# Other start addresses for the tiles that TensorE's split products read

## The chip, the core and the metric

The kernel runs as one program on one core of a Trainium2 chip. The metric is the device time of one execution in microseconds, the median of several executions. The core's engines are TensorE (PE, matrix products; its weight loads are listed apart, as PEld), VectorE (DVE), ScalarE (ACT), GpSimd (POOL) and SyncE (SP, which issues the large DMAs). SBUF is the on-chip memory that the engines read; in each of its 128 partitions a tile begins at a byte address, which the program's allocator sets when the program is built.

## What is computed

Three transformer-like blocks, one after the other, on 256 tokens of width 1024 in float32. Cut to the products that matter here:

```python
# block 1, twice: feed-forward, mixer (chunked_sgu or pool_mixer), feed-forward
x = x + 0.5 * (silu(rmsnorm(x) @ w_gate) * (rmsnorm(x) @ w_up)) @ w_out     # 1024 -> 2816 -> 1024
x = x + (u * gate(v)) @ w_out            # chunked_sgu: u, v = split(gelu(rmsnorm(x) @ w_in))
x = x + (grouped(pooled(p)) * scale) @ w_out      # pool_mixer: p = rmsnorm(x) @ w_in
# block 2: attention (two kinds), then a mixture of experts, 32 experts, 4 for each token
x = x + gt1 * rms_norm(concat(y_mla, y_dsa) @ w_o)
x = x + gt2 * rms_norm(moe_ffn(h2, w_router, w_mlp1, w_mlp2))
# block 3: stick-breaking attention and state-space branch, cross attention, convolution feed-forward
x = x + rms_norm(merged @ w_out)
x = x + rms_norm(memory_cross_attention(h, mem_n) )
x = x + rms_norm((gelu(gate) * val) @ w_down)     # gate, val = split(conv(h @ w_up)), 1024 -> 2816 -> 1024
```

## The kernel before

**Split products.** Outside the experts, a float32 product is made of three TensorE products of type float32r. Each operand is split into a high part (rounded, by ScalarE, line 163 or 192) and a low part (what is left, by VectorE, line 164 or 193). `mm3` (line 178) multiplies high by high, high by low, and low by high, into one PSUM bank:

```python
mm(out, whi, xhi, start=start, stop=False, skip_group_check=True)     # line 180
mm(out, whi, xlo, start=False, stop=False, skip_group_check=True)     # line 181
mm(out, wlo, xhi, start=False, stop=stop, skip_group_check=True)      # line 182
```

The first operand is loaded into the array as weights (128 x 128), the second moves past it (128 x 256, one column for each token). Every product has a weight load of its own. There are 3,862 calls of `mm3`, so 11,586 products; all but 246 of them have 256 columns.

**Where the operands lie.** `xhi` and `xlo` (the normalised input of a stage, 8 pieces of 256 columns each) are in the pool `const` from line 43 on, and stay at one place for the whole program. A stage's weights come by DMA into `rawp` (10 slots of 8 KB a partition) and are split into a tile `hi` of 8 KB from the ring `splitp` (`parts`, line 309): high part in the first half, low part in the second. Some stages add ring slots on the right-hand end of SBUF, in the pool `splitr` (`rings`, line 68). What the first layer of a feed-forward stage leaves is split into small tiles `ahi` and `alo` (128 x 256) from a pool that the stage opens itself, so their address depends on what was allocated before it: `ffna` in `ffn`, `sgu3` in `sgu`, `pm3` in `pool_mixer`, `mx1` in `mix3`, `xa2` in `cross`, `cv` in `conv_ffn`. A tile of weights and a piece of `xhi` are multiples of 512 bytes long, so within a stage a product's two addresses, taken modulo 512, are the same for every piece.

**Order.** A feed-forward stage takes one column tile of 128 of the hidden layer after the other: 48 products with `xhi`, `xlo` as the moving operand (8 pieces, gate and up, three each), then 24 with `ahi`, `alo` of an earlier tile (8 column tiles of the output, three each). The weights of the tiles to come are split meanwhile. The order on TensorE is that of the program; it does not depend on addresses. Every 36 to 70 us in block 1's feed-forward stages a side job (line 692, part of block 2's conditioning) puts other products between two tiles.

Of the kernel before, what the change touches and what calls it, by code (L numbers as in the profile page):

```python
# [12 lines left out]
F32 = mybir.dt.float32  # L13
F32R = mybir.dt.float32r
# [5 lines left out]
P = 128  # L20
T = 256
D = 1024
KT = D // P
# [18 lines left out]
class Net:  # L42
    def __init__(self, ctx, tc, I):
        self.ctx, self.tc, self.nc, self.I = ctx, tc, tc.nc, I
        self.uid = 0
        pool = lambda name, bufs, **kw: ctx.enter_context(tc.tile_pool(name=name, bufs=bufs, **kw))
        self.const = pool("const", 1)
        self.psum = pool("psum", 8, space=PSUM)
        self.small = pool("small", 2)
        self.rawp = pool("rawp", 10, reuse_waits="tile")  # L50
        self.ring_size, self.ring_scope, self.right_scope, self.latest = None, None, None, ()
        self.rings(8)
        nc = self.nc
        self.ident = self.const.tile([P, P], F32, name="ident")
        make_identity(nc, self.ident)
        self.ones = self.const.tile([P, 1], F32, name="ones")
        nc.vector.memset(self.ones, 1.0)
        self.mhalf = self.const.tile([P, 4], F32, name="mhalf")
        nc.vector.memset(self.mhalf, -0.5)
        self.xT = self.const.tile([P, KT, T], F32, name="xT")  # L60
        self.xhi = self.const.tile([P, KT, T], F32R, name="xhi")
        self.xlo = self.const.tile([P, KT, T], F32R, name="xlo")
# [5 lines left out]
    def rings(self, split, right=0, left=0):  # L68

        if self.right_scope is not None:  # L70
            self.right_scope.close()
        self.right_scope = ExitStack()
        if self.ring_size != split:
            if self.ring_scope is not None:
                self.ring_scope.close()
            self.ring_size = split
            self.ring_scope = ExitStack()
            if split:
                self.splitp = self.ring_scope.enter_context(self.tc.tile_pool(name=self.nm("splitp"), bufs=split, reuse_waits="tile"))
        self.turn_of = [self.splitp] * split  # L80
        for n, side in ((right, "right"), (left, "left")):
            if n:
                more = self.right_scope.enter_context(self.tc.tile_pool(name=self.nm("splitr"), bufs=n, reuse_waits="tile", side=side))
                self.turn_of += [more] * n

    def nm(self, s):
        self.uid += 1
        return f"{s}_{self.uid}"
# [220 lines left out]
    def parts(self, a, b, slot=False):  # L309
        if slot:  # L310
            t = self.slot(F32R).rearrange("p (z n) -> p z n", z=2)
        else:
            self.turn_of.append(self.turn_of.pop(0))
            t = self.turn_of[-1].tile([P, 2, 1024], F32R, tag="hi", name=self.nm("hi"))
        return tuple(t[:, z, :a * b].rearrange("p (a b) -> p a b", a=a) for z in range(2))

    def ahead(self, makers, n):
# [79 lines left out]
    def ffn(self, w_in, w_out, nxt, side, pieces=False, ready=(), fill=()):  # L397
        nc = self.nc
        F = D_FF // P
        wave = 2  # L400
        with self.tc.tile_pool(name=self.nm("ffna"), bufs=3) as ap_:
            raw, W, WO = {}, {}, {}

            def fetch(c):
# [97 lines left out]
    def sgu(self, w_in, w_s, b_s, w_out, vg, nxt):  # L502
        nc = self.nc
        A2 = 2048
        with self.tc.tile_pool(name=self.nm("sgu1"), bufs=1) as p1, \
                self.tc.tile_pool(name=self.nm("sgu3"), bufs=3) as p3:
            v = [self.slot() for _ in range(2)]
            bs = p1.tile([P, 8, P], F32, name=self.nm("bs"))
            nc.gpsimd.dma_start(bs, b_s.partition_broadcast(P))
# [20 lines left out]
            for c in range(4):  # L530
                pv = [self.bank(), self.bank()]
                for u in range(4):
                    hi, lo = get()
# [58 lines left out]
    def pool_mixer(self, w_in, w_grp, scale, w_out, nxt):  # L592
        nc = self.nc
        Z = 16
        with self.tc.tile_pool(name=self.nm("pm1"), bufs=1) as p1, \
                self.tc.tile_pool(name=self.nm("pm3"), bufs=3) as p3:
            inv = p1.tile([P, 4, Z], F32, name=self.nm("inv"))
            for g in range(4):
                w = 2 << g
# [77 lines left out]

    def ada_jobs(self, scratch, c, w, b, mod):
        nc = self.nc
        sc = self.const.tile([P, KT], F32, name=self.nm("sc"))  # L680

        parts = scratch.tile([4, 48, P], F32, name=self.nm("parts"))

        def job(i):
            if i == 0:
                nc.scalar.activation(sc, c(), AF.Silu)
            ps = self.bank()
            for q in range(2):
                raw = self.raw(w[512 * q:512 * (q + 1), 512 * i:512 * (i + 1)], 4, 512)
                for z in range(4):  # L690
                    k = 4 * q + z
                    nc.tensor.matmul(ps[32 * z:32 * z + 32, :], sc[:, k:k + 1].to_broadcast([P, 32]), raw[:, z, :],
                                     start=q == 0, stop=q == 1, tile_position=(0, 32 * z), skip_group_check=True)
            row = self.small.tile([P, 512], F32, tag="adarow", name=self.nm("adarow"), bufs=1)
            nc.scalar.copy(row, ps)
            for z in range(4):
                nc.gpsimd.dma_start(parts[z:z + 1, 4 * i:4 * i + 4, :].rearrange("z r m -> z (r m)"), row[32 * z:32 * z + 1, :])

        got = []

        def load():
            rows = self.small.tile([48, 4, P], F32, tag="adarow", name=self.nm("adarows"), bufs=1)
            got.append(rows)
            nc.gpsimd.dma_start(rows, parts.rearrange("z r m -> r z m"))

        def end():

            pt, rows = self.bank(), got[0]
            for z in range(4):
                nc.tensor.matmul(pt[:, 0:48], rows[:, z, :], self.ident[0:48, 0:48], start=z == 0, stop=z == 3, skip_group_check=True)  # L710
            nc.vector.tensor_tensor(mod, pt[:, 0:48], b(), op=ALU.add)

        return [lambda i=i: job(i) for i in range(12)] + [load, end]
# [1329 lines left out]
    def mix3(self, V, w_in, w_glu, w_a, w_s, w_out, nxt, units, ahead):  # L2043
# [3 lines left out]
        xhi, xlo = lambda k: self.xhi[:, k, :], lambda k: self.xlo[:, k, :]  # L2047
        with self.tc.tile_pool(name=self.nm("mx1"), bufs=1, reuse_waits="tile") as p1, \
                self.tc.tile_pool(name=self.nm("mx4"), bufs=2, reuse_waits="tile") as pg:
            so = p1.tile([P, 2, 4, T], F32R, name=self.nm("so"))  # L2050
            ao = p1.tile([P, 2, 4, T], F32R, name=self.nm("ao"))
            rb, r2 = None, None
            wg, gt = {}, {}
            with self.tc.tile_pool(name=self.nm("mx2"), bufs=1, reuse_waits="tile") as q1, \
# [182 lines left out]
                for i0 in (0, 2):  # L2237
                    hi, lo = self.unit(raws["glu"][:, :, i0 * P:(i0 + 2) * P])
# [65 lines left out]
    def cross(self, V, wq, wo, nxt, units, ahead):  # L2304
        nc = self.nc
        mm = nc.tensor.matmul
        with self.tc.tile_pool(name=self.nm("xa1"), bufs=1, side="right", reuse_waits="tile") as p1, \
                self.tc.tile_pool(name=self.nm("xa2"), bufs=2) as p2:
            self.rings(4, 1)
            mk = p1.tile([P, KT, T], F32, name=self.nm("mk"))  # L2310
            nc.sync.dma_start(mk, self.mk)
# [62 lines left out]
    def conv_ffn(self, V, w_up, w_down, nxt, units):  # L2374
# [3 lines left out]
        wave = 2  # L2378
        cw, cb = V["conv_w"], V["conv_b"]
        with self.tc.tile_pool(name=self.nm("cv"), bufs=3) as ap_:  # L2380
            raw, W, WO, gu, A = {}, {}, {}, {}, {}

            for i, unit in enumerate(units):
# [468 lines left out]
```

## Time and profile before

| | |
|---|---|
| median of 3 executions | 2688.53 us (2688.33 to 2691.99) |
| the profiled execution, its own time | 2696.91 us |
| its span, first to last instruction | 2695.2 us |
| mean granted TensorE clock | 0.948 of full speed |
| TensorE busy | 2443.8 us, 91% of the span |
| weight loads busy | 1863.6 us |
| VectorE, ScalarE, GpSimd busy | 1343.3, 918.1, 254.0 us |
| DMA | 716.20 MB, mean 266 GB/s |

How it is read: the span falls into stages. From 0 to 985 us are block 1's feed-forward stages and mixers, to 1210 us block 2's attention, to 2180 us the experts, to 2440 us the first part of block 3, to 2500 us its cross attention, and then the convolution stage. A TensorE row's busy time overlaps the next one's, because products are pipelined; what a product takes from the stage is the step from its start to the next one's start, which is read from the rows in order of time.

### The profile page before, as it was taken

Reading aid. Unit: us, or ns where it says so; the run is one execution under the profiler, and the core shown is the slowest. Engines: PE = TensorE matmul, PEld = TensorE weight load, DVE = VectorE, ACT = ScalarE, POOL = GpSimd, SP = SyncE. Lnnn points to the kernel's source line nnn. Section 1 sums busy time; section 2 is a strip of 40 time slices with the busy share of each in tenths; the row PEclk is TensorE's granted clock in tenths of the full one; section 3 lists DMA queues with packets and bytes.
Section 4 is the critical chain, followed back from the end, with each engine's and each line's share of the span. In section 5 each row is a group of like instructions: output and inputs, shape, how many; then the busy total and the mean of one; then the engine's idle time right before and its main releaser. Section 6 shows DMA issues by size and latency. Waiting matters only on the chain. (4 is left out here: it accounts for less than half of the span.)

```text
span 2695.2 us, 42836 instructions
## 1 busy us (share of the span) xinstructions
PE 2443.8 (91%) x17207; PEld 1863.6 (69%) x17207; DVE 1343.3 (50%) x2786; ACT 918.1 (34%) x1531; POOL 254.0 (9%) x444
## 2 busy tenths in 40 slices
PE   7999999999999999999889888789777787999998
PEld 7998999999999998784333333223222156998997
DVE  5556677577777775942111111111111059766875
ACT  4445454454445444531100100001010042555653
POOL 0011000110021102220000000000000027111000
PEclk8999999999999999999989989899999798999999
DMA  7956455676737652449999999999999973444640
GB/s 240 325 181 201 158 195 196 211 254 219 235 126 266 207 178 97 142 183 367 419 413 420 416 415 418 420 420 419 420 419 419 419 268 110 157 162 136 218 142 17
DMA packets 274116, 716.20 MB, mean 266 GB/s; under 512 B 15023, under 2 KB 179354, under 8 KB 223610
## 3 DMA queue, kind: packets, MB, share of 16 engines
q1 hardware_dynamic: 269370, 703.63, 69.8%
q0 software_dynamic: 4544, 9.80, 1.1%
q8 instruction: 136, 2.23, 0.3%
q14 instruction: 66, 0.54, 0.1%
HBM read 703.84 MB, written 9.54 MB: 265 GB/s over the span
## 5 line engine op out<-in xcount | busy, mean ns | idle before, releaser
L182 PE MATMUL b<-xhi,hi 128*128 128x256 f32 x2392 | 681.5, 285 | 15.7 <-DVE hi L164 15.6
L180 PE MATMUL b<-xhi,hi 128*128 128x256 f32 x2392 | 685.9, 287 | 6.0 <-ACT xhi L192 4.9
L181 PE MATMUL b<-xlo,hi 128*128 128x256 f32 x2392 | 680.8, 285 | 4.6 <-DVE xlo L193 2.4
L164 DVE TENSOR_TENSOR hi<-raw,hi 128x1024 fp32r<-128x1024 f32 (+3 forms) x517 | 605.9, 1184 | 157.5 <-ACT hi L163 152.7
L163 ACT CAST hi<-raw 128x1024 fp32r<-128x1024 f32 (+3 forms) x517 | 509.7, 1003 | 510.4 <-PE b L182 458.4
L180 PEld LDWEIGHTS b<-xhi,hi 128*128 128x128 f32 x2392 | 460.3, 192 | 19.5 <-ACT hi L163 7.8
L182 PEld LDWEIGHTS b<-xhi,hi 128*128 128x128 f32 x2392 | 460.1, 192 | 18.2 <-DVE hi L164 18.0
L181 PEld LDWEIGHTS b<-xlo,hi 128*128 128x128 f32 x2392 | 460.3, 192 | 6.5 <-DVE xlo L193 4.5
L1477 DVE TENSOR_SCALAR g<-b 128x256 f32<-128x256 f32 x48 | 20.3, 422 | 596.1 <-PE b L1496 331.8
L180 PE MATMUL b<-ahi,hi 128*128 128x256 f32 x1072 | 303.4, 284 | 1.8 <-ACT ahi L163 1.7
L181 PE MATMUL b<-alo,hi 128*128 128x256 f32 x1072 | 302.3, 282 | 2.2 <-DVE alo L164 1.3
L182 PE MATMUL b<-ahi,hi 128*128 128x256 f32 x1072 | 301.7, 282 | 0.0
L181 PEld LDWEIGHTS b<-alo,hi 128*128 128x128 f32 x1072 | 203.4, 190 | 3.2 <-DVE alo L164 2.2
L180 PEld LDWEIGHTS b<-ahi,hi 128*128 128x128 f32 x1072 | 203.1, 190 | 3.0 <-ACT ahi L163 2.9
L182 PEld LDWEIGHTS b<-ahi,hi 128*128 128x128 f32 x1072 | 203.5, 190 | 0.0
L1480 ACT ACTIVATE sg<-g 128x256 f32<-128x256 f32 x48 | 20.0, 416 | 525.5 <-DVE g L1477 525.5
L1528 PE MATMUL b<-raw,xe 128*64 128x512 f32 x648 | 153.1, 609 | 16.6 <-DMA raw<-in_w_mlp_dram 16.6
L1496 PE MATMUL b<-raw,xe 128*32 128x512 f32 x928 | 124.9, 650 | 35.3 <-DMA raw<-in_w_mlp_dram 35.0
L1577 ACT COPY y<-b 64x512 f32<-64x512 f32 x68 | 39.4, 579 | 249.4 <-PE b L1570 241.6
L1528 PEld LDWEIGHTS b<-raw,xe 128*64 128x64 f32 x648 | 42.6, 138 | 118.1 <-issue 74.4
L452 DVE TENSOR_TENSOR t<-b,rb 128x256 f32<-128x256 f32 x88 | 37.1, 422 | 167.2 <-PE b L182 167.1
L1496 PEld LDWEIGHTS b<-raw,xe 128*32 128x32 f32 x928 | 24.1, 112 | 118.6 <-DMA raw<-in_w_mlp_dram 75.7
(662 smaller groups left out, 3278.7 us busy)
## 6 DMA issues: line engine op xcount, KB each, us to landing
raw<-in_w_mlp_dram SPq DMA_DIRECT2D x275, 1024.0 KB
wb<-in_w_mlp_dram SPq DMA_DIRECT2D x108, 1024.0 KB
raw<-in_ffn_w_in_dram SPq DMA_DIRECT2D x84, 1024.0 KB
raw<-in_ffn_w_out_dram SPq DMA_DIRECT2D x44, 1024.0 KB
raw<-in_w_ada_dram SPq DMA_DIRECT2D x24, 1024.0 KB
raw<-in_ffn_w_up_dram SPq DMA_DIRECT2D x22, 1024.0 KB
raw<-in_w_in_dram SPq DMA_DIRECT2D x21, 1024.0 KB
raw<-in_a_w_in_dram SPq DMA_DIRECT2D x16, 1024.0 KB
```

What stands on the lines that cost most here:

```text
L163: a = self.nc.scalar.copy(hi, src)
L164: return a.ins, self.nc.vector.tensor_tensor(lo, src, hi.bitcast(F32), op=ALU.subtract).ins
L180: mm(out, whi, xhi, start=start, stop=False, skip_group_check=True)
L181: mm(out, whi, xlo, start=False, stop=False, skip_group_check=True)
L182: mm(out, wlo, xhi, start=False, stop=stop, skip_group_check=True)
L452: nc.vector.tensor_tensor(t, ps[:, :T], rb, op=ALU.mult)
L1477: nc.vector.tensor_scalar(g, v[:, :, 0], 7.0, None, op0=ALU.min)
L1480: nc.scalar.activation(sg, g, AF.Sigmoid, scale=1.702)
L1496: mm(ps[32 * c:32 * c + 32, :], xe(k), chunk(w[k][:, 0, :], c), start=False, stop=k == KT - 1, tile_position=(0, 32 * c), skip_group_check ...
L1528: mm(pq[q][64 * b:64 * b + 64, :], xe(k), chunk(w[:, 0, :], 2 * q + b), start=False, stop=k == KT - 1, tile_position=(0, 64 * b), skip_gro ...
L1577: nc.scalar.copy(y[64 * z:64 * z + 64, 512 * c:512 * c + 512], py[64 * c:64 * c + 64, :])
```

## The change

The instructions stay as they are. The two built programs hold the same instructions in the same order on each engine, with the same operands and shapes; on TensorE and SyncE the semaphore waits are the same too, and 12 instructions on ScalarE, VectorE and GpSimd have a wait more or less, where two tiles now overlap differently in SBUF. What differs is where tiles begin:

- `sc`, 32 bytes, came later in the pool `const` and is now allocated ahead of `xT`, `xhi` and `xlo`, so these three lie 32 bytes higher.
- A new function `shift` allocates an unused tile. In the pools of the stages it stands ahead of the others (64 to 192 bytes, as the stage needs it), and in the ring on the right-hand end it takes 448 bytes.

Below, the distance is the address of the moving operand less that of the weights, modulo 512. After the change it is 192 in nearly all of these products (seen from the weights' side: 320).

| moving operand, weights | products | moving, mod 512 | weights, mod 512 | distance |
|---|---|---|---|---|
| `xhi`, `xlo` of all stages, `hi` (24 of them `raw`) | 6,675 | 192 -> 224 | 32 | 160 -> 192 |
| `xhi`, `xlo`, `hi` of the right ring (convolution stage) | 504 | 192 -> 224 | 480 -> 32 | 224 -> 192 |
| `ahi`, `alo` of `ffn`; `so`, `ao`, `mhi`, `mlo` of `mix3` | 2,496 | 32 -> 224 | 32 | 0 -> 192 |
| `ahi`, `alo` of `sgu` | 384 | 64 -> 224 | 32 | 32 -> 192 |
| `ahi`, `alo` of `pool_mixer`, of `conv_ffn` (left ring); `yhi`, `ylo` of `cross` (left ring) | 600 | 160 -> 224 | 32 | 128 -> 192 |
| `ahi`, `alo` of `conv_ffn`, `yhi`, `ylo` of `cross` (right ring) | 312 | 160 -> 224 | 480 -> 32 | 192 -> 192 |
| `hi` moving, 512 columns, `xhi`, `xlo` as weights (`sgu`, `mix3`) | 240 | 32 | 192, now 224 | 352 -> 320 |
| slots of `rawp` and other tiles | 354 | as before | as before | as before |
| router's products | 21 | 192 -> 224 | several | several |

```diff
+        self.sc = self.const.tile([P, KT], F32, name="sc")
         self.xT = self.const.tile([P, KT, T], F32, name="xT")
@@ rings
+        self.shifts = {}
         for n, side in ((right, "right"), (left, "left")):
...
+                if side == "right":
+                    self.shifts[more] = 448
+    def shift(self, pool, n):
+        pool.tile([P, n // 4], F32, tag="shift", name=self.nm("shift"), bufs=1)
@@ parts
-            t = self.turn_of[-1].tile([P, 2, 1024], F32R, tag="hi", name=self.nm("hi"))
+            pool = self.turn_of[-1]
+            t = pool.tile([P, 2, 1024], F32R, tag="hi", name=self.nm("hi"))
+            if pool in self.shifts:
+                self.shift(pool, self.shifts.pop(pool))
@@ ffn
+            self.shift(ap_, 192)
@@ sgu
+            self.shift(p3, 160)
@@ pool_mixer
+            self.shift(p3, 64)
@@ ada_jobs
-        sc = self.const.tile([P, KT], F32, name=self.nm("sc"))
+        sc = self.sc
@@ mix3
+            self.shift(p1, 192)
@@ cross
+            self.shift(p2, 64)
@@ conv_ffn
+            self.shift(ap_, 64)
```

## Rows read from the trace of the kernel before

**Rows 1.** The page, busy time of each engine, share of the span, instructions

```profile
PE 2443.8 (91%) x17207; PEld 1863.6 (69%) x17207; DVE 1343.3 (50%) x2786; ACT 918.1 (34%) x1531; POOL 254.0 (9%) x444
```

**Rows 2.** Groups by line: count | busy us, mean ns | idle before, releasers

```profile
L180 PE MATMUL b<-xhi,hi 128*128 128x256 f32 x2392 | 685.9, 287 | 6.0 <-ACT xhi L192 4.9 <-ACT xhi L912 1.1
L182 PE MATMUL b<-xhi,hi 128*128 128x256 f32 x2392 | 681.5, 285 | 15.7 <-DVE hi L164 15.6
...
L180 PE MATMUL b<-ahi,hi 128*128 128x256 f32 x1072 | 303.4, 284 | 1.8 <-ACT ahi L163 1.7
...
L180 PE MATMUL b<-hi,xhi 128*128 128x512 f32 x80 | 32.6, 407 | 0.0
```

**Rows 3.** Busy time by stretch: us, each engine, PEclk, DMA share, GB/s

```profile
0.00:221.00 221.00, 205.88 (x1683) 198.10 (x1684) 122.53 (x169) 100.10 (x140) 18.96 (x32) 0.97 0.76 247
...
276.00:384.00 108.00, 107.93 (x903) 107.61 (x902) 75.37 (x113) 49.69 (x75) 4.67 (x3) 0.98 0.52 174
384.00:580.00 196.00, 195.36 (x1646) 189.43 (x1644) 133.36 (x292) 91.41 (x133) 14.28 (x67) 1.00 0.65 219
...
1210.00:2180.00 970.00, 800.30 (x4202) 298.95 (x4203) 147.88 (x446) 97.10 (x191) 2.60 (x4) 0.91 1.00 410
...
2500.00:2695.20 195.20, 182.47 (x1515) 179.43 (x1513) 138.16 (x244) 98.97 (x157) 10.85 (x45) 0.97 0.35 118
```

**Rows 4.** TensorE in order of time, first feed-forward stage: start us, busy us, instruction

```profile
136.05 0.39 PE L180 MATMUL b<-xhi,hi 128*128 128x256 f32 x1
136.27 0.28 PE L181 MATMUL b<-xlo,hi 128*128 128x256 f32 x1
...
141.85 0.28 PE L180 MATMUL b<-ahi,hi 128*128 128x256 f32 x1
...
144.72 0.28 PE L180 MATMUL b<-xhi,hi 128*128 128x256 f32 x1
...
150.35 0.28 PE L180 MATMUL b<-ahi,hi 128*128 128x256 f32 x1
...
153.22 0.28 PE L180 MATMUL b<-xhi,hi 128*128 128x256 f32 x1
```

**Rows 5.** TensorE in order of time, cross attention, output product (shorter steps)

```profile
2467.79 0.28 PE L181 MATMUL b<-ylo,hi 128*128 128x256 f32 x1
...
2470.28 0.28 PE L182 MATMUL b<-yhi,hi 128*128 128x256 f32 x1
```

**Rows 6.** TensorE in order of time, cross attention, output product (longer steps)

```profile
2449.48 0.36 PE L180 MATMUL b<-yhi,hi 128*128 128x256 f32 x1
2449.68 0.28 PE L181 MATMUL b<-ylo,hi 128*128 128x256 f32 x1
...
2452.27 0.28 PE L182 MATMUL b<-yhi,hi 128*128 128x256 f32 x1
```

**Rows 7.** TensorE in order of time, gated mixer, output product

```profile
367.39 0.28 PE L182 MATMUL b<-ahi,hi 128*128 128x256 f32 x1
...
372.75 0.28 PE L180 MATMUL b<-xhi,hi 128*128 128x256 f32 x1
```

**Rows 8.** TensorE in order of time, pool mixer, output product

```profile
807.78 0.28 PE L180 MATMUL b<-ahi,hi 128*128 128x256 f32 x1
...
816.33 0.28 PE L180 MATMUL b<-raw,hi 128*128 128x256 f32 x1
```

**Rows 9.** TensorE in order of time, convolution stage, weights from the right ring

```profile
2568.64 0.28 PE L180 MATMUL b<-xhi,hi 128*128 128x256 f32 x1
...
2574.19 0.28 PE L182 MATMUL b<-xhi,hi 128*128 128x256 f32 x1
```

**Rows 10.** TensorE in order of time, third block, at the lower clock

```profile
2256.30 0.41 PE L180 MATMUL b<-xhi,hi 128*128 128x256 f32 x1
...
2259.07 0.40 PE L181 MATMUL b<-xlo,hi 128*128 128x256 f32 x1
```

## The prediction

> **What bounds the kernel now.** I read the page first. TensorE is busy for 91% of the span, VectorE for half of it [rows 1]. The stretches say where that matters: in the feed-forward stages and the gated mixer TensorE is busy for 93 to 100% of the stretch at a granted clock of 0.97 to 1.00, with the DMA engines at 0.76 or less; among the experts DMA is at 1.00, and TensorE waits for it [rows 3]. The split products are 11,586 instructions in the stages of the first kind, and the time that TensorE idles in front of the largest groups of them is small, 6.0 and 15.7 us over 2,392 products each [rows 2]. So outside the experts the time is the number of split products times the step from one start to the next.
>
> That step is read from the rows in order of time, not from the busy time (280 ns for each product, pipelined). In the first feed-forward stage, 48 products with xhi, xlo take from 144.72 to 150.35 us, 117.3 ns a step; the 24 with ahi, alo that follow take until 153.22, 119.6 ns a step; and the 47 from 136.27 to 141.85 take 118.7 ns [rows 4]. At 2.4 GHz, 256 columns at one a cycle are 106.7 ns, so 11 to 13 ns a step are something else. At the lower level of the clock, 1.2 GHz, 13 steps take 2.77 us, 213.1 ns each, which is 256 columns and nothing on top [rows 10]. The excess belongs to the full clock alone.
>
> **What the change does to a step.** It removes no instruction and adds none; only the distance between the two operands' addresses (moving less weights, modulo 512) changes. The trace of before already holds six distances with 256 columns, and their steps are not alike:
> - distance 0 (2,496 products): 119.6 ns [rows 4];
> - 32 (384): 46 steps in 5.36 us, 116.5 [rows 7];
> - 128 (600): 72 steps in 8.55 us, 118.7 [rows 8];
> - 160 (6,675): two patterns, 117.3 and 118.7 [rows 4]; I take the middle, 118.0, since both recur through all stages;
> - 224 (504): 47 steps in 5.55 us, 118.1 [rows 9];
> - 192 (312): two patterns again, but farther apart: 22 steps in 2.49 us, 113.2 [rows 5], and 22 steps in 2.59 us, 117.7 [rows 6].
>
> These 10,971 products have a mean of 118.3 ns, and after the change all of them are at distance 192. What they then cost is bounded by the two patterns of that distance. With each step at 113.2 the gain is 10,971 x 5.1 = 56 us; with each at 117.7 it is 10,971 x 0.6 = 6.6 us. Of either I keep 0.96, since in these stretches the clock is granted to 0.97 to 1.00 [rows 3], a step at the lower clock has nothing to lose [rows 10], and a few steps lie beside waits: 53.6 and 6.3 us. One ns a step is worth 10.5 us.
>
> **Which of the two patterns.** Of the 18 stretches of at least five steps at this distance, 11 settle at 113 to 114 ns and 7 at 117 to 118, within five steps, and once settled none leaves its pattern before the distance changes or a wait comes. After the change the distance no longer alternates between 48 steps of one kind and 24 of another, so a pattern can last from one wait to the next: whatever a restart falls into is then paid for hundreds of products. There is one restart behind a gap at this distance: a step of 200 ns at 2449.48, and it falls into the long pattern [rows 6]. But restarts are of two kinds. That one leaves a step of 200 to 206 ns, as the starts of stages and the gated mixer's units do; behind a side job the step is 220 ns or more (136.05 to 136.27 [rows 4]), and at distance 160 this second kind mostly falls into the other pattern than the first. Most of a feed-forward stage comes behind the second kind, for which distance 192 has no row. I therefore take half of the products in each pattern: 115.4 ns, a gain of 2.84 x 10.5 = 30 us.
>
> **The rest of the change.** 240 products with 512 columns go from distance 352 to 320, for which there is no row. The spread over all distances is 6.5 ns for 256 columns, so at most 13 for 512: 240 x 13 = 3 us either way, taken as 0; their group is small [rows 2]. The waits that differ are 12, none of them on TensorE or SyncE: taken as 0. Nothing of the experts' 970 us gets shorter, where the DMA is full [rows 3]; they only start earlier by what the stages ahead of them gain. Should TensorE get faster, VectorE and ScalarE must keep the pace with their splits: in the second feed-forward stage they are busy for 133 and 91 of 196 us [rows 3], so a step 3 to 4% shorter leaves both with cover.
>
> **The sum.** The profiled execution took 2696.9 us (span 2695.2): 2666.9 after. The median shown is 8.4 us lower; with the same gain, 2688.5 - 29.9 = 2658.6.
>
> **The rivals.**
> 1. *All short.* Each restart falls into 113 ns: 2688.5 - 53.6 = 2634.9. For it: 11 of 18. Against: the one restart seen.
> 2. *All long.* 2688.5 - 6.3 = 2682.2, on the border of what can be told. For it: that restart. It would need the second kind of restart to do the same.
> 3. *The address does not matter.* The steps then differ for another reason (the source of the moving operand, or the splits that run beside them), and nothing moves: 2688.5. Against it: xhi, xlo and yhi, ylo show several steps each when only the distance differs, and two patterns occur at one distance with the same operands. The Trainium skill states this rival (SBUF — State Buffer, section Who interferes with whom: TensorE's reads for the moving operand and for the weights have ports that are independent, and only VectorE and GpSimd share one; TensorE: Matmul & The Clock Gate, section Step-by-step: what each phase is for: loading the next weights takes no read bandwidth from the running matmul). By that rule the sum would be zero; the trace does not agree, with 119.6 ns against 113.2 for the same shape.
> 4. *Slower: the places count, not their distance.* All 312 products at distance 192 have weights at 480 and the moving operand at 160. Weights at 32 with a moving operand at 224 occur nowhere in the trace. The longest steady step with weights at 32 is 119.6 ns; at that step the cost is 10,971 x 1.3 x 0.96 = 14 us: 2702. It is slower from a new step above 118.3 on. For it: all short steps have weights at 480. Against: distance 224 has weights at 480 too and takes 118.1 ns [rows 9], so that place is not what makes a step short.
> 5. *The gain is lost elsewhere*, in a wait for the splits or a DMA that TensorE then meets: 2688. The cover above speaks against it.
>
> **How the numbers follow.** Both patterns mixed, 0.60; all short, 0.13; all long, 0.12; address without effect, 0.05; slower, 0.08; lost elsewhere, 0.02. About 0.2%, 5.4 us, is what a measurement of this kernel can tell from no change. Faster: 0.60 + 0.13 + 0.07 of the all-long case = 0.80; within: 0.05 of that case, 0.05 and 0.02 = 0.12; slower: 0.08. The range goes from all short to just past all long, 2635 to 2684, and leaves out the address without effect, the slower case, the lost gain and the far edges of the first two, some 0.2.
>
> **What would show it.** In the profile of the changed kernel the steps of xhi, xlo and of ahi, alo in a feed-forward stage must be equal, where they were 117.3 to 118.7 and 119.6 [rows 4]; 113 or 118 in long unbroken stretches, with a change of pattern at a wait only, is right. The gated mixer, which restarts with the first kind every 6 us, should stay near 118 and gain little; the experts keep their 970 us. The prediction is wrong if steps of another size appear at this distance, if one pattern takes all, or if TensorE's idle time grows in front of line 180 to 182.

## The result and the profile after

The changed kernel takes 2658.93 us, median of 4 executions (2655.45 to 2663.34), beside 2689.06 for the kernel before on the same chip: a ratio of 0.9887, 95% interval 0.9874 to 0.9900. The forecast was 2659.0. The profiled execution took 2658.7 us, its span 2657.0.

The groups of TensorE by line in the changed kernel (its `mm3` has lines 188 to 190, where before had 180 to 182); columns as in [rows 2]:

```profile
L188 PE MATMUL b<-xhi,hi 128*128 128x256 f32 x2392 | 677.6, 283 | 6.4 <-ACT xhi L200 5.3 <-ACT xhi L926 1.1
L190 PE MATMUL b<-xhi,hi 128*128 128x256 f32 x2392 | 673.0, 281 | 14.8 <-DVE hi L172 14.7
...
L188 PE MATMUL b<-ahi,hi 128*128 128x256 f32 x1072 | 299.0, 280 | 2.8 <-ACT ahi L171 2.8
...
L188 PE MATMUL b<-hi,xhi 128*128 128x512 f32 x80 | 31.6, 395 | 0.0
```

Each group is as large as in [rows 2], a product is 4 ns shorter, and the idle time ahead of the groups is what it was: 6.4 and 14.8 us against 6.0 and 15.7. So nothing is won or lost at a wait; TensorE goes through the same work in shorter steps. The stretches (columns as in [rows 3]: us, busy time of PE, PEld, DVE, ACT, POOL, granted clock, DMA share, GB/s) show it too:

```profile
276.00:384.00 108.00, 107.92 (x930) 107.55 (x929) 75.21 (x109) 54.17 (x79) 6.22 (x4) 1.00 0.58 193
384.00:580.00 196.00, 195.09 (x1680) 188.95 (x1680) 136.33 (x294) 91.07 (x132) 15.79 (x68) 1.00 0.67 223
```

TensorE fills the same 108 and 196 us as before [rows 3], with 930 and 1,680 instructions in place of 903 and 1,646; in the second stretch VectorE rises from 133 to 136 us, far from its limit.

The steps are read in order of time (start us, busy us, instruction). Two stretches of feed-forward stages, each from its first product to the side job that ends it:

```profile
597.39 0.39 PE L188 MATMUL b<-xhi,hi 128*128 128x256 f32 x1
597.61 0.28 PE L189 MATMUL b<-xlo,hi 128*128 128x256 f32 x1
...
662.68 0.28 PE L190 MATMUL b<-ahi,hi 128*128 128x256 f32 x1
662.89 0.64 PE L706 MATMUL b<-raw,sc 128*32 128x512 f32 x4
```

```profile
398.71 0.38 PE L188 MATMUL b<-xhi,hi 128*128 128x256 f32 x1
398.93 0.28 PE L189 MATMUL b<-xlo,hi 128*128 128x256 f32 x1
...
432.61 0.28 PE L190 MATMUL b<-ahi,hi 128*128 128x256 f32 x1
432.82 0.64 PE L706 MATMUL b<-raw,sc 128*32 128x512 f32 x4
```

A step is the time from one product's start to the next one's, and a pattern is a run of equal steps. From 597.61 to 662.68 lie 574 steps, 113.4 ns each; from 398.93 to 432.61 lie 286 steps, 117.8 ns each. In both, products with xhi, xlo and with ahi, alo alternate every 48 and 24 instructions, and the step does not change, where before it went from 117.3 to 119.6 and back [rows 4]. All 10,869 steps of split products with 256 columns at the full clock, added up from the trace, have a mean of 114.80 ns (before: 10,839 with 118.30). Those at distance 192 have 114.66, which is what 70% of them in a pattern of 113.3 ns and 30% in one of 117.8 ns give. The two sums, 1282.3 and 1247.8 us, are over unequal counts. Taken product by product, the 10,837 steps that are under 140 ns in both traces took 1281.5 us before and 1243.5 after: 38.0 us less, where the span is 38.2 us shorter. Everything else, waits included, adds up to almost nothing.

Where the gain arises, from the start of the same split product in both traces: the changed kernel leads by 6.9 us at product 1,600 (before 225.5 us), 15.6 at 4,000 (555.7), 29.4 at 7,600 (1015.7), 31.8 at 9,000 (2328.6), 37.8 at 11,000 (2607.4). It grows with the number of split products and stands still in the experts: product 8,000 to 9,000 took 1243.7 us before and 1243.3 after.

### The profile page after: what moved, and what is told of

Its sections match the earlier page's. It is cut to its first block, busy times and chain, and to the rows that moved or that the text cites. A ratio compares the mean times of both kernels' runs of the same rounds, so it can differ in the third digit from the quotient of the medians.

```text
span 2657.0 us, 42833 instructions
## 1 busy us (share of the span) xinstructions
PE 2409.7 (91%) x17207; PEld 1826.7 (69%) x17207; DVE 1342.1 (51%) x2786; ACT 915.8 (34%) x1531; POOL 254.4 (10%) x444
## 5 line engine op out<-in xcount | busy, mean ns | idle before, releaser
L190 PE MATMUL b<-xhi,hi 128*128 128x256 f32 x2392 | 673.0, 281 | 14.8 <-DVE hi L172 14.7
L188 PE MATMUL b<-xhi,hi 128*128 128x256 f32 x2392 | 677.6, 283 | 6.4 <-ACT xhi L200 5.3
L189 PE MATMUL b<-xlo,hi 128*128 128x256 f32 x2392 | 672.7, 281 | 4.6 <-DVE xlo L201 2.5
L188 PE MATMUL b<-ahi,hi 128*128 128x256 f32 x1072 | 299.0, 280 | 2.8 <-ACT ahi L171 2.8
L190 PE MATMUL b<-ahi,hi 128*128 128x256 f32 x1072 | 297.3, 278 | 0.8 <-DVE hi L172 0.8
L1510 PEld LDWEIGHTS b<-raw,xe 128*32 128x32 f32 x928 | 24.4, 113 | 118.5 <-DMA raw<-in_w_mlp_dram 75.1
```

The costliest lines, as they stand in the source:

```text
L1510: mm(ps[32 * c:32 * c + 32, :], xe(k), chunk(w[k][:, 0, :], c), start=False, stop=k == KT - 1, tile_position=(0, 32 * c), skip_group_check ...
```

## The experiments

**A map of the steps.** The kernel `map32` is TensorE all but alone: ScalarE is busy for 3% of its span, the other engines and the DMA for next to nothing. It repeats stretches of 45 products at one distance, eight for each: four behind ordinary float32 products (`other`) and four behind one split product whose weights ScalarE writes (`fresh`). Behind `other` the first step is 220 to 232 ns. Ahead of `fresh` and behind it TensorE does not pause, so those four stretches follow on from the ones before. None of the network is computed.

```diff
+    def stretch(self, name, d, at, n=45, mix=None):
+        ps = self.bank(name)
+        for i in range(n):
+            wa = at // 4 + 128 * (i % 8)
+            xa = (at // 4 + (d if mix is None or i >= mix[1] else mix[0]) // 4) % 128 + 256 * (i % 8)
+            self.product(ps, self.w[:, wa:wa + P], self.x[:, xa:xa + T], i == 0, i == n - 1)
```

> It leaves out the whole computation and writes a constant: TensorE alone runs, stretches of 45 products of 128x128 by 256 columns, 8 stretches for each of 28 cases (names atDx: weights at one place, moving operand D bytes further modulo 512; placeAx: distance 192 with the weights A bytes further on; ledDx: distance 192 with 6 products at distance D ahead of each stretch). Theory, the distance decides: the distances that the kernel before has repeat their steps here, 0 near 120 ns, 32 near 116.7, 128 near 118.6, 160 at 117.3 or 118.7, 192 at 113.3 or 117.8, 224 near 118.2, and distance 192 takes 113.3 or 117.8 at all eight places; the ten other distances lie between 113 and 120. Rival, the places count: distance 192 takes other steps at some of the eight places. Rival, the other engines' reads make the excess: with TensorE alone all distances take the same step. The led cases: if the state at the switch sets the pattern, the four stretches behind one kind of restart all settle alike.

Rows of TensorE in order of time; a row is one stretch of 45 products, its busy time the 44 steps and 0.28 us for the last product. The name holds the distance (`place224x`: distance 192 with the weights at 224):

```profile
103.09 5.56 PE L71 MATMUL at0x<-x,w 128*128 128x256 f32 x45
...
154.28 5.42 PE L71 MATMUL at32x<-x,w 128*128 128x256 f32 x45
...
382.21 5.39 PE L71 MATMUL at192x<-x,w 128*128 128x256 f32 x45
...
389.36 5.57 PE L71 MATMUL at192x<-x,w 128*128 128x256 f32 x45
...
511.14 5.56 PE L71 MATMUL at256x<-x,w 128*128 128x256 f32 x45
...
562.33 5.42 PE L71 MATMUL at288x<-x,w 128*128 128x256 f32 x45
...
1042.38 5.38 PE L71 MATMUL place224x<-x,w 128*128 128x256 f32 x45
...
1049.53 5.57 PE L71 MATMUL place224x<-x,w 128*128 128x256 f32 x45
```

At distance 0 a step is (5.56 - 0.28) / 44 = 120.0 ns, at 32 it is 116.8; 256 repeats 0 and 288 repeats 32 to the row. The same sum gives 116.1 and 120.2 ns for the rows of 5.39 and 5.57 us, which stand behind `other` and have a long first step in them; their last 24 steps have 113.3 and 117.8. Over the last 24, the steps are 120.0 ns at 0 and 96, 116.7 at 32, 113.3 or 117.8 at 64 and 192, 118.5 to 118.8 at 128, 117.2 to 118.8 at 160, 118.3 at 224; from 256 to 480 the same again. So the addresses alone do it, and what counts is the distance modulo 256, not 512. At distance 192 the two patterns come at every place of the weights that was tried. Which of the two comes does go with the place: in the four stretches behind `fresh` all are short with the weights at 32 or 160 modulo 256 and all long with them at 64 or 224, and places 256 bytes apart take the same pattern in each of their eight stretches. The rows of 5.39 and 5.57 us hold the same 45 products behind the same kind of start: the pattern is taken within the first steps and kept. Six products at distance 0 or 32 ahead of the stretch led to the short pattern 8 times of 8, six at 128 to the long one 8 times of 8.

**All products at distance 0.** `zero` is the changed kernel with the same tiles moved to other places, all of them to distance 0 (three more pools like the one shown; in two the `shift` is left out).

```diff
+        self.mod = self.const.tile([P, 48], F32, name="mod")
+        self.b_route = self.const.tile([P, 32], F32, name="b_route")
...
-            self.shift(p3, 160)
+            self.shift(p3, 480)
```

> The whole computation, with all tiles shifted so that moving operand and weights lie at distance 0 (11,000 of the split products). Theory, the distance decides: each step is 119.8 to 120 ns where before it is 118.3 on average, so 1.5 to 1.7 x 10.5 = 16 to 18 us slower than before: about 2706 us. Rival, addresses do not matter: 2689 us, steps as before.

```profile
619.16 0.39 PE L190 MATMUL b<-xhi,hi 128*128 128x256 f32 x1
619.38 0.28 PE L191 MATMUL b<-xlo,hi 128*128 128x256 f32 x1
...
688.25 0.28 PE L192 MATMUL b<-ahi,hi 128*128 128x256 f32 x1
```

It took 2705.14 us beside 2686.82 for the kernel before: ratio 1.0069 (1.0052 to 1.0086), slower by 18 us. The 574 steps between the two rows take 120.0 ns each (the same 574 products as at 597.61 above), and the mean over 10,943 is 120.00. Taken product by product, the steps cost 17.9 us more than before. The same edit, with other numbers in it, makes the kernel slower by the steps of the map: the cause is not that the tiles moved, but the distance that they moved to.

**The two halves of the change.** `const_only` moves `sc`, and with it `xhi` and `xlo`; `pools_only` does the rest (the shifts of the stages' pools and of the right ring). Both are shown against the changed kernel, `const_only` first.

```diff
-                    self.shifts[more] = 448
+                    pass
...
-            self.shift(ap_, 192)
```

```diff
-        self.sc = self.const.tile([P, KT], F32, name="sc")
...
-        sc = self.sc
+        sc = self.const.tile([P, KT], F32, name=self.nm("sc"))
```

> The change's first part alone: xT, xhi and xlo 32 bytes higher, all other tiles as before. Distance 192 for 6,675 products with xhi and xlo, 0 still for the 24 products with ahi and alo between them, 256 for the 504 of the right ring. Theory, the distance decides and the state at a switch sets the pattern: the 48 steps with xhi and xlo take 113.4 to 114 or 117.8 after a short run-in, the 24 with ahi and alo 119.7; since each stretch is entered from the same state, most stretches of a stage behave alike. Gain between 1 and 30 us; at the share of the whole change (7 in 10 short) 20 us: 2669. Rival, addresses do not matter: 2689.

> The other part alone: the tiles ahi, alo, so, ao, mhi, yhi and the right ring shifted, xhi and xlo where they were. Distance 192 for 3,800 products, 160 for those with xhi and xlo. Theory: the 24 steps with ahi and alo take 113.4 to 114 or 117.8, those with xhi and xlo 117.3 or 118.7 as before; at 7 in 10 short the gain is 3,480 products x 4.5 ns x 0.96 = 15 us, between 4 and 20: 2674. If the two parts add up, the gains of the two runs sum to the 30 us of the whole change; if long unbroken stretches at one distance are worth more, their sum is less. Rival, addresses do not matter: 2689.

`const_only` took 2672.42 us (2671.38 to 2675.92), ratio 0.9941 (0.9924 to 0.9957); `pools_only` 2675.57 (2675.21 to 2677.7), ratio 0.9956 (0.9940 to 0.9973). The two gains are 0.59 and 0.44%, together 1.03%, against 1.13% for the whole, the same within the intervals: the change is its two halves, and neither is idle. (By the steps alone, product by product, the halves gain 21.1 and 19.9 us, and the whole 38.0.) A feed-forward stage of `const_only`, where 48 products are at 192 and 24 at 0:

```profile
139.35 0.28 PE L188 MATMUL b<-ahi,hi 128*128 128x256 f32 x1
...
142.22 0.29 PE L188 MATMUL b<-xhi,hi 128*128 128x256 f32 x1
142.34 0.28 PE L189 MATMUL b<-xlo,hi 128*128 128x256 f32 x1
...
147.68 0.28 PE L188 MATMUL b<-ahi,hi 128*128 128x256 f32 x1
```

The 24 take 119.6 ns each, the 48 take 113.8: whenever it follows 24 at distance 0, a stretch of 48 at 192 settles in the short pattern in this trace, as behind six products at 0 in the map.

**A finer map.** `map8` does the same in steps of 8 bytes, with 48 products a stretch. It also puts one to three products at distance 0 at the head of stretches at 192, and changes the distance of one to six products in the middle of a stretch at 192. None of the network is computed.

```diff
-    ('at32x', 32, 32, None),
-    ('at64x', 64, 32, None),
...
+    ('at104x', 104, 32, None),
+    ('at112x', 112, 32, None),
...
+    ('kick0ax', 192, 32, (0, 20, 21)),
```

> It leaves out the whole computation and writes a constant, as the first map. Stretches of 48 products, 8 for each of 35 cases. atDx: distance D in steps of 8 bytes between the multiples of 32 already seen, from 8 to 248. Theory, the two reads meet in blocks: a distance of 8 or 16 bytes from a known one shifts its pattern gradually, steps between 113 and 120 ns, and near 64 and 192 both 113.3 and 117.8 occur; if one distance has the short pattern alone, all 8 of its stretches settle at 113.3. Rival, only whole 32-byte blocks count: 8, 16 and 24 bytes more give the steps of the multiple of 32 below. leadax to leadcx: distance 192 with the first 1, 2 or 3 products at distance 0; kickEax, kickEbx, kickEcx, kickEfx: distance 192 with 1, 2, 3 or 6 products at distance E from the 21st on. Theory, products at distance 0 or 32 set the state from which the short pattern is reached: with 6 of them all 8 stretches end at 113.3 though they may begin at 117.8; with 1 to 3 perhaps not all. Rival, the restart alone decides: about half of the stretches end at 117.8, kicked or not.

```profile
624.81 5.75 PE L78 MATMUL at112x<-x,w 128*128 128x256 f32 x48
...
653.05 5.65 PE L78 MATMUL at112x<-x,w 128*128 128x256 f32 x48
...
1224.72 6.17 PE L78 MATMUL at232x<-x,w 128*128 128x256 f32 x48
```

Most distances step at 118 to 122 ns, 232 at 123.3; 8, 16 or 24 bytes more do change a step, so blocks of 32 bytes are not the unit. One distance, 112, ends at 113.3 in all eight stretches, behind either kind of start (16 does so once of eight); its busy time of 5.65 us is 0.05 more than 47 steps of 113.3 and the last product, so the first steps are longer. Of the 64 stretches at 192 in which one, two, three or six products in the middle stand at 0 or 32, 32 stood in the long pattern ahead of these; 30 of them end in the short one, and 2 of the 32 short ones end in the long one. A pattern can be changed on the way by products at another distance, not only at a start. At the head, one, two and three products at distance 0 led to the short pattern in 6, 8 and 5 of eight: that few do not do it safely.

**Again, and at distance 112.** `after_again` is the changed kernel once more. `x112` puts `xhi` and `xlo` into one tile and begins them 16 bytes into it, so that 7,179 products stand at distance 112 modulo 256; the order on TensorE stays.

```diff
+        self.mod = self.const.tile([P, 48], F32, name="mod")
         self.xT = self.const.tile([P, KT, T], F32, name="xT")
-        self.xhi = self.const.tile([P, KT, T], F32R, name="xhi")
-        self.xlo = self.const.tile([P, KT, T], F32R, name="xlo")
+        xx = self.const.tile([P, 2 * KT * T + 8], F32R, name="xx")
+        self.xhi, self.xlo = (xx[:, 4 + z * KT * T:4 + (z + 1) * KT * T].rearrange("p (j t) -> p j t", j=KT) for z in range(2))
...
-                    self.shifts[more] = 448
+                    self.shifts[more] = 416
```

> The changed kernel itself once more, with a second profile, beside the two kernels that put the products at another distance. The first theory (a stretch of products at distance 192 falls into the 113.3 ns pattern or the 117.8 ns pattern when it starts, and keeps it to the next wait, by the state of the moment) allows the share of the two to differ a little from execution to execution: 2655 to 2663 us, mean step 114.4 to 115.0 ns against 114.66 in the first profile. The rival, that the pattern is fixed by the program (which instructions stand ahead of the stretch), gives the same stretches the same pattern as in the first profile: the gated mixer 46 steps at 113.6 and 46 at 117.8 in turn, the stretches of 286 steps at 398.9, 507.2 and 2558.8 us long again.

> xhi and xlo are moved by 16 bytes more, so that 7179 of the split products stand at distance 112 modulo 256 in place of 192; the 3,500 others keep 192, and the order of the instructions on TensorE is that of the changed kernel. The map of the steps by 8 bytes gave 113.3 ns in all eight stretches at 112. If the distance alone sets the step, the products of xhi and xlo all step at 113.3 ns in place of a mean of 114.66: 1.33 ns by some 6,850 at the full clock is 9 us, so 2646 to 2653, and the gated mixer runs at 113.3 throughout. Rival: the 112 of the map was its eight stretches' luck, and in the kernel, behind other restarts, it takes the slow pattern of its neighbours 104 and 120 (120 ns and more): 5.3 ns by 6,850 is 37 us more, 2695. A second rival: something other than the address (the supply of weights, the clock) holds the mean near 114.7: 2657 to 2661, no change from the changed kernel.

`after_again` took 2656.87 us (2649.88 to 2658.52), ratio 0.9882 (0.9860 to 0.9903), with a mean step of 114.57 at distance 192; one execution lies below the 2655 to 2663 us expected. But its stretches are not the same as in the first profile. The same 287 products there, and here:

```profile
506.96 0.39 PE L188 MATMUL b<-xhi,hi 128*128 128x256 f32 x1
507.19 0.28 PE L189 MATMUL b<-xlo,hi 128*128 128x256 f32 x1
...
540.87 0.28 PE L190 MATMUL b<-ahi,hi 128*128 128x256 f32 x1
```

```profile
508.63 0.38 PE L188 MATMUL b<-xhi,hi 128*128 128x256 f32 x1
508.85 0.28 PE L189 MATMUL b<-xlo,hi 128*128 128x256 f32 x1
...
541.26 0.28 PE L190 MATMUL b<-ahi,hi 128*128 128x256 f32 x1
```

The first are 286 steps of 117.8 ns, the second 286 of 113.3. Of the 65 stretches of 30 steps and more that both profiles hold, 53 have the same pattern in both, 7 went from short to long and 5 from long to short. So the program alone does not fix the pattern. It goes in part with the first step: in both profiles together, of 62 stretches that follow a first step of 219 to 230 ns, 47 are short (five of five at 226 are long), and of 60 that follow one of 200 to 206, 27 are short. A first step of 222 ns led to either pattern in the map. What decides at a restart is left open.

`x112` took 2653.18 us (2649.39 to 2655.98), ratio 0.9861 (0.9838 to 0.9885): 3.7 us less than `after_again`, where 9 were expected; the two intervals overlap, so the times do not tell the two kernels apart; what differs is read from the steps. A feed-forward stage of it:

```profile
111.06 0.28 PE L189 MATMUL b<-ahi,hi 128*128 128x256 f32 x1
...
113.78 0.29 PE L189 MATMUL b<-xx,hi 128*128 128x256 f32 x1
113.91 0.29 PE L190 MATMUL b<-xx,hi 128*128 128x256 f32 x1
114.04 0.28 PE L191 MATMUL b<-xx,hi 128*128 128x256 f32 x1
...
119.30 0.28 PE L189 MATMUL b<-ahi,hi 128*128 128x256 f32 x1
```

The 24 products at 192 now step at 113.3 ns, always, since they come from 112 (ahi's mean over the program falls from 114.52 to 113.67). The 48 at 112 take 115.0: each change from 192 to 112 costs two steps of 130 ns and then some at 119 before the pattern is reached, 73 ns a time, and in the gated mixer, where 23 follow each change, the mean is 116.5. Distance 112 reaches its pattern from every start seen here, but not at once; the mean of its products is 114.77, no better than 192.

**Distance 112 for both.** `all112` puts ahi and alo of the five feed-forward stages at 112 too, in one tile of three pairs written in turn. As written, the first pair is written again before the products that read it, so the output of these stages is not the network's; only its steps and waits are read here. `all112b` writes it behind them.

```diff
-            self.shift(ap_, 192)
+            self.shift(ap_, 96)
+            pairs = self.pairs(ap_)
...
-                hi = ap_.tile([P, T], F32R, tag="ahi", name=self.nm("ahi"))
-                lo = ap_.tile([P, T], F32R, tag="alo", name=self.nm("alo"))
+                hi, lo = pairs[j % 3]
```

```diff
-                    act(j, rb)
+                    if j > wave + 1:
+                        act(j, rb)
                 for i in range(j - wave if j > wave + 1 else 0, j - wave + 1):
                     if i < F - TAIL:
                         self.acc_feed(acc, WO.pop(i), A.pop(i), i == 0, False)
+                    if i == 0:
+                        act(j, rb)
```

> As the last, and ahi and alo of the five feed-forward stages at distance 112 too, in one tile of three pairs in place of a pool's three buffers (some products of the last units of a stage then stand a few places earlier or later). 9,800 of the 10,900 split products are at 112. If the distance alone sets the step: another 1.33 ns by some 2,500 products at the full clock, 3.4 us, so 2643 to 2650 and a mean step of 113.4 to 113.6. If 112 takes the slow pattern: 2705. If the pairs' one tile adds waits (a product of a pair must be done before the pair is written again), idle time ahead of the products of ahi and alo shows it, and the time stays near that of the kernel with xhi and xlo alone.

> As all112, with the first pair of each feed-forward stage written again only behind the products that read it: each stage computes as in the changed kernel, and the instructions on TensorE, VectorE and ScalarE stand in the order of the changed kernel. 9,800 of the 10,900 split products are at distance 112, so the change from 192 to 112 at each turn from ahi to xhi, which cost a stretch of xhi in x112 some 73 ns each time (two steps of 127 and 130 ns and then 119 before 113.3), is gone in those stages. If 112 settles into 113.3 from wherever it starts: a mean step of 113.6 to 114.0 at the full clock against 114.7, 0.9 ns by 10,870 is 10 us less than the changed kernel, 2645 to 2650. If the steps are that short and the time is still 2655 or more, the gain is taken by something else, and the idle time ahead of products or the granted clock shows where (all112 lost 24 us ahead of the first products of ahi and 0.02 of clock behind them).

`all112` took 2680.82 us (ratio 0.9966, 0.9955 to 0.9977), although its mean step is 114.0. By line, and in the first feed-forward stage (in brackets the idle time before the row and what ended it):

```profile
L194 PE MATMUL b<-ahi,hi 128*128 128x256 f32 x1072 | 299.4, 282 | 26.4 <-ACT ahi L177 26.4
```

```profile
48.95 0.58 PE L194 MATMUL b<-ahi,hi 128*128 128x256 f32 x1 [3.59 <-ACT ahi L177]
```

TensorE waits 26.4 us ahead of ahi, in place of 2.8, because the first feed now has to wait for a split of a later tile, and behind the wait the clock is at its lower level. The stretch from there on (us, busy time of PE, granted clock, DMA share, GB/s):

```profile
48.90:52.00 3.10, 3.05 (x14) 0.51 1.08 360
```

A granted clock of 0.51 is the level of 1.2 GHz; before it TensorE had idled from 45.37 to 48.95. Shorter steps were worth less than one misplaced wait a stage.

`all112b` has the order of the changed kernel on TensorE, VectorE and ScalarE, and took 2646.30 us (2642.45 to 2650.64), ratio 0.9837 (0.9822 to 0.9852), inside the 2645 to 2650 expected. A feed-forward stage of it:

```profile
112.90 0.28 PE L194 MATMUL b<-xx,hi 128*128 128x256 f32 x1
113.01 0.28 PE L195 MATMUL b<-xx,hi 128*128 128x256 f32 x1
...
118.34 0.28 PE L194 MATMUL b<-ahi,hi 128*128 128x256 f32 x1
```

The 48 products take 113.3 ns each, and so do the 24 that follow; the mean of all steps is 113.99. It is faster than the changed kernel by 10.6 and 12.6 us (medians of `after_again` and of the first result), and its interval lies below that of either. Product by product, the steps account for about 8 of that, 7.7 and 8.6 us against the two profiles.

**Which two operands meet.** In `pairs` the weights lie at 32 and 160 in turn, the moving operand at a fixed distance from its own weights. None of the network is computed.

```diff
+            turn = 0 if mix is None else 128 * (2 * (i % mix[0]) // mix[0])
+            wa = (at + turn) // 4 % 128 + 128 * (i % 8)
+            xa = (at + turn + d) // 4 % 128 + 256 * (i % 8)
```

> TensorE alone in stretches of 48 products with 256 columns; none of the network is computed. The weights of the products lie at 32 and at 160 modulo 256 in turn, the moving operand of each at a fixed distance from its own weights, so that a product's distance to its own weights and its distance to the weights of the next product differ by 128. First theory: what counts is the moving operand against the next product's weights, which are loaded while it runs. Then the steps at 0 and 128 change places against the map by 32 bytes: own distance 128 steps at 120.0 ns and own distance 0 at 118.4 to 118.7; own 96 (next 224) at 118.3, own 224 at 120.0; own 160 (next 32) at 116.7, own 32 at 117.2 to 118.7; own 240 (next 112) settles at 113.3, own 112 at 117.2. Rival: what counts is the distance to the product's own weights; then own 0 is 120.0, own 112 settles at 113.3 and so on, as in the maps. In the cases named two, the weights change place at each second product only, so that the next product's weights are at the own distance and at 128 from it in turn, and the weights after the next always at 128 from it: by the first theory the steps alternate between two kinds, with a mean between those of the two distances; if the weights two products ahead counted, the steps would be those of the own distance plus 128 throughout.

Rows of TensorE in order of time, one stretch of 48 products each:

```profile
109.43 5.77 PE L61 MATMUL own0x<-x,w 128*128 128x256 f32 x48
...
377.32 5.91 PE L61 MATMUL own224x<-x,w 128*128 128x256 f32 x48
```

Both theories fell. With the weights in turn, the own distances 0, 128, 32, 160, 96, 112, 64 and 192 all step at 116.7 ns; only 224 (120.0) and 240 (120.0, once 116.7) differ. With the weights changing place at each second product only, the steps are 118.3 ns at own distances 0, 32, 160 and 112, 117.5 or 118.3 at 96, 117.2 at 240 and (once 118.3) at 128, and 120.0 at 224. At 0 that is less than at either of the distances that occur in it, 120.0 (0) and at least 118.5 (128), so no mean of the map's steps gives it. Neither the distance to the own weights nor that to the next ones sets the step by itself. The map by distance holds where all products of a stretch have the same places modulo 256; which accesses meet in TensorE's reads is left open.

## Why the prediction was right, point by point

**The bound.** That the stages outside the experts are the number of split products times their step held: the steps took 38.0 us less of a span that fell by 38.2, idle time ahead of the groups stayed, and `zero` moved the time the other way by 18 us, with steps that cost 17.9.

**The sum.** Right in its mechanism; that it met the median within 0.1 us is luck. The term that was mis-sized is the step. The forecast was 115.4 ns, from half of the products in each pattern, and a gain of 30 us; measured is 114.8, since 70% were in the short one, and a gain of 38.0 us by the steps. With that gain the sum would have been 2650.5. What brought the median back to the forecast was not in the sum: the medians moved by 30.1 us only (27 to 34 by the ratio's interval), and by 34.4 in the second comparison, with `after_again`. The two profiled executions do lie 38.2 us apart, but that of before, at 2696.91 us, stood 7.9 above the median of its kernel. Two profiles of the changed kernel differ by 8.8 us in span (2657.0, 2648.2), of which the steps make 0.9 and the stretch between products 8,000 and 9,000, in the experts, 6. So a few us between two executions say nothing about the change, and why the medians moved by less than the steps is left open.

**Which pattern.** Long unbroken patterns that change at waits only are there (574 steps in one). The two kinds of restart do differ, but neither decides alone. The first, 200 to 206 ns, was taken from one stretch as long [rows 6], and is short in 27 of 60 stretches (of 30 steps and more, in two profiles). The second, for which there was no row and behind which most of a feed-forward stage comes, is short in 47 of 62: hence 70% in place of half. The forecast that the gated mixer, which restarts with the first kind, "should stay near 118 and gain little" failed:

```profile
279.63 0.28 PE L189 MATMUL b<-alo,hi 128*128 128x256 f32 x1
...
284.85 0.28 PE L190 MATMUL b<-xhi,hi 128*128 128x256 f32 x1
...
285.53 0.28 PE L189 MATMUL b<-alo,hi 128*128 128x256 f32 x1
...
290.95 0.28 PE L190 MATMUL b<-xhi,hi 128*128 128x256 f32 x1
```

One unit of the changed kernel's mixer has 46 steps of 113.5 ns, the next 46 of 117.8, and so on in turn, in both profiles; the lead over the kernel before grows by 5.4 us between product 1,600 and 2,500, which is mostly this stage.

**Modulo 512.** The measure itself was too wide: the map repeats after 256 bytes. No distance of the sum was named wrongly by it, since 320 and 64, 352 and 96 concern the 240 products of 512 columns alone.

**What was taken as nothing.** The products with 512 columns went from 233.3 to 229.2 ns a step (mean busy time 407 [rows 2] to 395), a gain of 1 us where 0, 3 either way, stood. The waits of other engines and the cover of VectorE and ScalarE are as forecast, and so is the experts' stage.

**The rivals.** All short did not happen by itself; distance 112 in `all112b` comes near its step (113.99 ns), at 2646.30 us. All long did not happen. That the address does not matter is excluded by the map and by `zero`. The Trainium skill (SBUF — State Buffer, section Who interferes with whom) gives TensorE two independent read ports, for the moving operand and for the weights; a reader would take from that that the addresses of the two cannot matter. The map does not bear that reading out, with 113.3 to 123.3 ns for one shape and TensorE all but alone. That the places count in place of their distance is excluded too, as far as the size of a step goes: weights at nine places give the same two at 192. Which of the two is taken does go with the place in the map. Gain lost elsewhere: not here, but `all112` shows what it looks like.

## What to carry to other kernels

Where TensorE runs one product after the other with a weight load for each, read the step from start to start, by the operands' addresses modulo 256; steps of 113 to 123 ns lay in the choice here, and allocation decides it unseen. Measure a map of the steps with TensorE alone before choosing, look at how a stretch starts and not at its steady state only, and prefer one distance for all products of a stage, since a change of distance can cost longer steps for a while (73 ns a time from 192 to 112). Check that the padding which moves a tile does not move a wait with it: one misplaced wait a stage, with the lower clock behind it, ate 34 us.

## What was not expected

One program takes different patterns in different executions: 12 of 65 stretches changed between two profiles of the changed kernel, by 4.4 ns for each of up to 286 steps. At distance 112 the short pattern is reached from every start that was tried, at a cost of some 73 ns a time behind 192; at 192 and 64 it is a matter of the start and of what stood ahead. And weights that alternate between two places 128 bytes apart step at 116.7 ns at nearly any distance, so a distance is no property of two operands alone.
